# First feed-forward block: pairs 0 to 8 for each group alone, 9 to 21 for both groups by seven block products; three more convolution tiles on TensorE; the sums of one layer norm on VectorE

## The chip, the cores and the metric

One of the cores of a Trainium2 chip runs one inference step of a speech-encoder trunk. The metric is device time in microseconds (us) of one execution. The median of three runs before the change is 1541.64 us (1540.84 to 1542.74). One more execution was recorded by the profiler.

Engines: PE is TensorE (matrix products; its weight loads are shown as PEld), DVE is VectorE, ACT is ScalarE, POOL is GpSimd, SP is SyncE, which here only issues DMAs.

## The reference

640 columns (frames) of 1024 features: 128 of eight running streams ("sample") and 512 of one new stream ("prompt"). Layer 0 is a convolution module and a SwiGLU feed-forward block (FFN); layer 1 is attention on a shared key and value and a second FFN. What the change touches is layer 0:

```python
def swiglu_ffn(h, g, w_in, w_out):
    a, b = jnp.split(rms_norm(h, g) @ w_in, 2, axis=-1)
    return h + (jax.nn.silu(a) * b) @ w_out

def conv_module(h, hist, g, w_pw1, b_pw1, w_dw, b_dw, ln_g, ln_b, w_pw2, b_pw2):
    a, gate = jnp.split(rms_norm(h, g) @ w_pw1 + b_pw1, 2, axis=-1)
    glu = a * jax.nn.sigmoid(gate)
    full = jnp.concatenate([hist.astype(glu.dtype), glu], axis=1)
    y = lax.conv_general_dilated(
        full, w_dw[:, None, :].astype(full.dtype), window_strides=(1,), padding="VALID",
        dimension_numbers=("NWC", "WIO", "NWC"), feature_group_count=D_MODEL) + b_dw
    y = jax.nn.silu(layer_norm(y, ln_g, ln_b))
    return h + y @ w_pw2 + b_pw2, full[:, -CONV_HIST:]
```

The depthwise convolution has 31 taps. The hidden width is 2816 = 22 x 128, so an FFN has 22 "pairs": a pair is one 128-wide tile of `a` and the tile of `b` beside it, and needs 1 MB of `w_in`.

## The kernel before, in words

Features lie on the 128 partitions (8 tiles of 128), frames in the free dimension. The 640 columns are two groups: g0, the first 256 (the sample and 128 of the prompt), and g1, the other 384. Each group goes through the convolution module and the first FFN by itself, so that g0's FFN can run on PE while g1 is still in its convolution.

**Products.** All matrices are fp32, split in a high part `whi`/`xh` and a low part `wlo`/`xl`. `mm3` (L173) makes three matmuls for every 128x128 block: whi with xh, wlo with xh, whi with xl (L176 to L178). `wsplit` (L132) loads one weight tile of up to 1 MB through SP's queue, ACT copies it to `whi` (L156), and `wlo` = raw - `whi` is made at L160, by DVE, or by DVE and POOL: with pool=n, n quarters on POOL. `whi` and `wlo` have two buffers each. The raw tile has two buffers ("raw"), and every third load goes to a buffer of its own ("rx", tile pool `rxs`).

**FFN.** `ffn` (L327) runs chunks of pairs. `ffn_in` (L277) makes the two products of a pair and the gate, which leaves `hid` in both parts; after a chunk, `ffn_out` (L311) multiplies `hid` by the matching rows of `w_out`, and `out_tile` adds the result to the residual `h`. `FS` holds the chunks that g0 does alone: pairs 0 to 5, 6 to 11, 12 to 17. `FC` is the chunk for both groups with one weight tile (18 to 21). `FD` holds g1's chunks alone (0 to 17 once more, with the weights loaded a second time).

**Order of the convolution module.** The string `PLAN` (L72) is read token by token. Each token emits a step, the digit behind its letter is the group, the next ones are feature tiles: a and b make pw1 with GLU; l loads a convolution tile and p computes it on PE (`conv_pe_load` L448, `conv_pe` L465: 32 matmuls with 32 columns of weights; the input goes to DRAM as `sc` and comes back as `x4` through SP's queue; `w4` and `x4` have one buffer); d computes convolution tiles on DVE (`conv` L426, a scalar_tensor_tensor for each tap at L443, its accumulator in PSUM); q computes one by ACT's multiplies and POOL's adds (`conv_pool` L404, L422/L423); n is the layer norm over features (`conv_ln` L480); w is pw2; r is the RMS norm ahead of the FFN (`rms_late` L254); s writes convolution state out; f is one of `FS`'s chunks for g0. A step that stands later in the program is later on every engine's queue, unless `high_priority` lets it go ahead.

**The layer norm.** `colmean` (L192) adds the eight tiles up elementwise (L201 on POOL), then PE sums over partitions (L210) and `spread` (L216, L222) brings the mean to all partitions in PSUM. `conv_ln` subtracts the mean, squares, and does the same again for the variance; then it multiplies (L495), applies SiLU and splits into the parts that pw2 (w) multiplies.

**The second FFN** already works otherwise from its fourth pair on. With the 1024 features in two halves and the 640 columns in two halves of 320, a pair is a product of 2x2 blocks (of the weights: a's and b's halves; of the input: B11 to B22). The class `Unit` makes it by seven block products m1 to m7 instead of eight, with sums of weight blocks made on DVE and POOL (`prep`) and sums of input blocks (T1 to T4) made once. Each block product is 12 matmuls of 320 columns, so a pair takes 84; results are collected in PSUM banks pa, pb, pc, two of each.

## Time and profile before

| | us |
|---|---|
| median of three runs | 1541.64 (1540.84 to 1542.74) |
| the profiled execution's own time | 1541.31 |
| span of the profiled execution, first to last instruction | 1539.5 |
| PE busy | 1467.9 (95% of the span) |
| DVE busy | 1049.0 (68%) |
| ACT busy | 667.1 (43%) |
| POOL busy | 447.3 (29%) |
| granted TensorE clock, mean | 0.988 |

The profile is one execution on the chip. A row of the timeline or of the chain of waits has start and length in us, engine, the destination tile and line, operation, operand tiles and shapes, and in brackets how long the engine had been idle and what released it. Matmuls are pipelined: their listed lengths overlap, so the cost of one in a stream is the distance of two starts divided by the steps between them. "busy" of PE is therefore not work done at full speed.

### The profile page before, as it was taken

Reading aid. Unit: us, or ns where it says so; the run is one execution under the profiler, and the core shown is the slowest. Engines: PE = TensorE matmul, PEld = TensorE weight load, DVE = VectorE, ACT = ScalarE, POOL = GpSimd, SP = SyncE. Lnnn points to the kernel's source line nnn. Section 1 sums busy time; section 2 is a strip of 40 time slices with the busy share of each in tenths; the row PEclk is TensorE's granted clock in tenths of the full one; section 3 lists DMA queues with packets and bytes.
Section 4 is the critical chain, followed back from the end, with each engine's and each line's share of the span. In section 5 each row is a group of like instructions: output and inputs, shape, how many; then the busy total and the mean of one; then the engine's idle time right before and its main releaser. Section 6 shows DMA issues by size and latency. Waiting matters only on the chain.

```text
span 1539.5 us, 27212 instructions
## 1 busy us (share of the span) xinstructions
PE 1467.9 (95%) x11054; PEld 1397.9 (91%) x11054; DVE 1049.0 (68%) x1890; ACT 667.1 (43%) x1196; POOL 447.3 (29%) x406
## 2 busy tenths in 40 slices
PE   5988898989999999999999999999999999999998
PEld 5878878988999999999988798896989999999998
DVE  6994999989555444556577767666796467467456
ACT  4544455545423323235455445343564144244144
POOL 6965458987401000001322111110421011011010
PEclk9989899999999999999999999999999999999999
DMA  7884334454421333432555545444103222222222
GB/s 261 249 219 143 123 103 162 146 183 151 151 83 56 123 123 123 126 120 96 196 184 195 170 151 199 150 158 151 32 25 117 76 83 89 76 83 90 76 83 83
DMA packets 57022, 200.54 MB, mean 130 GB/s; under 512 B 10176, under 2 KB 20672, under 8 KB 44096
## 3 DMA queue, kind: packets, MB, share of 16 engines
q1 hardware_dynamic: 56608, 198.48, 39.1%
q8 instruction: 87, 1.43, 0.4%
q10 hardware_dynamic: 288, 0.31, 0.1%
q14 instruction: 39, 0.32, 0.1%
HBM read 187.55 MB, written 11.22 MB: 129 GB/s over the span
## 4 chain that ended last, share of the span: by engine, by line
PE 73%; DVE 15%; issue 3%; ACT 3%; POOL 3%; DMA 3%; SPq 0%; POOLq 0%; ACTq 0%; DVEq 0%
PE mm L176 13%; PE mm L177 13%; PE mm L178 13%; PE pb L977 6%; DVE w L443 4%; PE pc L977 4%; DVE wlo L160 4%; PE pa L977 3%; PE w L803 1%; PE pb L176 1%; PE pb L178 1%; PE pb L177 1%; PE pa L178 1%; PE pa L176 1%; PE pa L177 1%
## 5 line engine op out<-in xcount | busy, mean ns | idle before, releaser
L177 PE MATMUL mm<-x,wlo 128*128 128x256 f32 (+1 forms) x1344 | 417.8, 313 | 15.8 <-DVE wlo L160 15.4
L176 PE MATMUL mm<-x,whi 128*128 128x256 f32 (+1 forms) x1344 | 414.4, 312 | 9.2 <-ACT x L165 6.9
L178 PE MATMUL mm<-x,whi 128*128 128x256 f32 (+1 forms) x1344 | 413.0, 311 | 2.5 <-DVE x L166 2.5
L177 PEld LDWEIGHTS mm<-x,wlo 128*128 128x128 f32 x1344 | 257.1, 191 | 19.4 <-DVE wlo L160 18.3
L176 PEld LDWEIGHTS mm<-x,whi 128*128 128x128 f32 x1344 | 255.1, 191 | 14.1 <-ACT x L165 7.7
L178 PEld LDWEIGHTS mm<-x,whi 128*128 128x128 f32 x1344 | 255.3, 191 | 5.2 <-DVE x L166 4.1
L156 ACT ACTIVATE whi<-raw 128x2048 fp32r<-128x2048 f32 (+2 forms) x87 | 143.9, 1658 | 171.9 <-PE mm L178 105.1
L160 DVE TENSOR_TENSOR wlo<-raw,whi 128x2048 fp32r<-128x2048 f32 (+5 forms) x87 | 156.4, 1801 | 44.7 <-ACT whi L156 44.0
L922 POOL TENSOR_TENSOR raw<-raw 128x512 f32<-128x512 f32 x38 | 56.4, 1485 | 326.4 <-DVE raw L922 255.2
L177 PE MATMUL mm<-hid,wlo 128*128 128x256 f32 (+1 forms) x352 | 107.6, 308 | 6.1 <-DVE wlo L160 6.1
L160 POOL TENSOR_TENSOR wlo<-raw,whi 128x1536 fp32r<-128x1536 f32 (+3 forms) x33 | 93.0, 2822 | 55.1 <-ACT whi L156 55.1
L178 PE MATMUL mm<-hid,whi 128*128 128x256 f32 (+1 forms) x352 | 105.8, 307 | 0.8 <-DVE hid L166 0.7
L443 DVE SCALAR_TENSOR_TENSOR w<-gp,dwv,w 128x384 f32<-128x384 f32 x180 | 104.4, 613 | 0.9
L176 PE MATMUL mm<-hid,whi 128*128 128x256 f32 (+1 forms) x352 | 104.4, 307 | 0.0
L201 POOL TENSOR_TENSOR acc<-sq,sq 128x384 f32<-128x384 f32 (+1 forms) x8 | 8.1, 1006 | 255.8 <-ACT sq L185 255.8
L156 ACT ACTIVATE whi<-rx 128x2048 fp32r<-128x2048 f32 (+1 forms) x30 | 54.0, 1800 | 54.0 <-PE mm L178 42.0
L177 PEld LDWEIGHTS mm<-hid,wlo 128*128 128x128 f32 x352 | 66.0, 188 | 7.1 <-DVE wlo L160 7.1
L160 DVE TENSOR_TENSOR wlo<-rx,whi 128x2048 fp32r<-128x2048 f32 (+4 forms) x30 | 62.9, 2098 | 13.3 <-ACT whi L156 12.4
L423 POOL TENSOR_TENSOR y<-y,cvt 128x256 f32<-128x256 f32 (+1 forms) x60 | 67.9, 1132 | 4.3 <-ACT cvt L422 2.2
L178 PEld LDWEIGHTS mm<-hid,whi 128*128 128x128 f32 x352 | 65.7, 188 | 1.2 <-DVE hid L166 1.2
L176 PEld LDWEIGHTS mm<-hid,whi 128*128 128x128 f32 x352 | 65.1, 188 | 0.3 <-ACT hid L165 0.3
L165 ACT ACTIVATE whi<-raw 128x1024 fp32r<-128x1024 f32 x38 | 39.4, 1054 | 54.2 <-DVE raw L922 19.1
(329 smaller groups left out, 3648.2 us busy)
## 6 DMA issues: line engine op xcount, KB each, us to landing
raw<-in_w_in SPq DMA_DIRECT2D x49, 1024.0 KB
raw<-in_w_out SPq DMA_DIRECT2D x28, 768.0 KB
cache<-in_ck SPq DMA_DIRECT2D x32, 512.0 KB
cache<-in_cv SPq DMA_DIRECT2D x32, 512.0 KB
raw<-in_w_pw SPq DMA_DIRECT2D x14, 1024.0 KB
rx<-in_w_in SPq DMA_DIRECT2D x13, 1024.0 KB
rx<-in_w_pw SPq DMA_DIRECT2D x8, 1024.0 KB
raw<-in_w_kq SPq DMA_DIRECT2D x8, 1024.0 KB
```

Source lines behind the costliest of these rows:

```text
L156: nc.scalar.activation(out=hi[:, a:b], in_=raw[:, a:b], func=AF.Copy)
L160: eng.tensor_tensor(out=lo[:, a:b], in0=raw[:, a:b], in1=hi[:, a:b].bitcast(F32), op=ALU.subtract)
L165: nc.scalar.activation(out=hi, in_=src, func=AF.Copy)
L176: nc.tensor.matmul(ps, wh, xh, start=(i == 0), stop=False)
L177: nc.tensor.matmul(ps, wl, xh, start=False, stop=False)
L178: nc.tensor.matmul(ps, wh, xl, start=False, stop=(i == last))
L201: last["acc"] = eng.tensor_tensor(out=acc[:, :n], in0=prev, in1=s(), op=ALU.add)
L423: nc.gpsimd.tensor_tensor(out=y[g][:, c, :], in0=y[g][:, c, :], in1=pr[:, :n], op=ALU.add)
L443: nc.vector.scalar_tensor_tensor(out=dst, in0=src, scalar=wj, in1=dst, op0=ALU.mult, op1=ALU.add)
L803: nc.tensor.matmul(st[32 * b:32 * b + 32, 0:512], qv[b], KC[b // 2][:, b % 2, :], start=True, stop=True)
L922: ENG[e].tensor_tensor(out=out, in0=a, in1=b, op=op)
L977: nc.tensor.matmul(ps, a[:, c], b[:, k, :], start=(first and k == 0 and i == 0), stop=(k == 3 and i == 2), skip_group_check=not first)
```

## The change

- `FS` is (0,4), (4,4), (8,1): g0 alone does pairs 0 to 8. `FD` is (0,5), (5,4): g1 alone does the same pairs. `FC` is (9,5), (14,4), (18,4): 13 pairs for both groups, now by `Unit`, which moves up in the program and takes the weight tensor as an argument. The host swaps the halves of the b rows for pairs 9 and up.
- In `PLAN` g1's tile 6 leaves ACT and POOL (q16) and its tiles 2 and 7 leave DVE (d127); all three go to PE: l12 ahead of b6, p12 and l17 behind it, p17 and l16 behind the second pair of g0's first chunk and p16 behind its fourth. Two of g0's three lone chunks now stand ahead of g1's pw2 where three stood.
- `conv_ln` takes its sums' engine from `LE`: POOL for g0 as before, DVE for g1.
- g1's RMS norm keeps the products of gain and `h` in a tile `xg` (`keep=xg`). While g1's lone chunks run, they are multiplied there by the norm's factor, g0's normed columns are put beside them (the sum of the two parts of its input), and the blocks B11, B21, T1 to T3 are made from `xg`; B22 and T4 are made behind those chunks. Their tiles, `xe0`, `a22`, `xg0`, `tq0`, are allocated when the convolution's pools are closed, and the third raw buffer (`rxs`) is given up there, not at the end of the FFN.
- `bank()` in the first FFN takes the tag "mm", which has four PSUM banks; the second FFN has six.
- g1's lone chunks split 3/4 of `wlo` on POOL (`PFB`, where pool was 0); g0's do as before.

```diff
-FS = ((0, 6), (6, 6), (12, 6))
-FC = ((18, 4),)
-FD = ((0, 6), (6, 6), (12, 6))
+FS = ((0, 4), (4, 4), (8, 1))
+FC = ((9, 5), (14, 4), (18, 4))
+FD = ((0, 5), (5, 4))
...
+CHC = 5
...
-PLAN = ("a0 y a1 a2 a4 x a3 a5 a6 l04 p04 l05 d0213 a7 b0 p05 b1 l07 p07 l06 b2 q00 s0 p06 n0 b3 b4 b5 d145 l13 w0 b7 r0 p13 b6 f q16 s1 d101 d127 n1 f f w1 r1")
+PLAN = ("a0 y a1 a2 a4 x a3 a5 a6 l04 p04 l05 d0213 a7 b0 p05 b1 l07 p07 l06 b2 q00 s0 p06 n0 b3 b4 b5 d145 l13 w0 b7 r0 p13 l12 b6 p12 l17 s1 d101 f1p17.1l16.3p16 n1 f w1")
...
-    def rms_late(g, gain, engs=SQ, cut=CUT):
+    def rms_late(g, gain, engs=SQ, cut=CUT, keep=None):
...
-                t = tp.tile([P, 384], F32, tag="n1", name=nm("n1"), bufs=NB1)
+                t = (tp.tile([P, 384], F32, tag="n1", name=nm("n1"), bufs=NB1) if keep is None
+                     else keep[:, k, GR[g][0]:GR[g][0] + n])
...
+    def bank(tag=None):
+        if stage[0] == 0:
+            return mmt()
...
+    def units(src, js, where, chunks, u, hids, new_hid, outs):
+        for j in js:
+            c, jj = where[j]
+            w = None
+            if j + 1 < FT:
+                w = Unit(src, j + 1, hids[c], where[j + 1][1])
+                w.prep()
+                w.m1()
+            u.m7()
+            if w:
+                w.m5()
+            u.m3()
+            u.m4()
+            if w:
+                w.m6()
+                w.m2()
...
+    LE = (nc.gpsimd, nc.vector)
...
-        r, v = colmean(mu, [lambda c=c: y[g][:, c, :] for c in order], n, LCUT, "mst")
+        r, v = colmean(mu, [lambda c=c: y[g][:, c, :] for c in order], n, LCUT, "mst", LE[g])
...
-        bc, _ = rstd_bc([y[g][:, c, :] for c in order], n)
+        bc, _ = rstd_bc([y[g][:, c, :] for c in order], n, eng=LE[g])
...
     cv.close()
+    rxs.close()
+    third[1] = None
...
+    xs0, xs1 = late[0], rms_late(1, V_NFFN, keep=xg)
+    ffn({0: hp0}, w_in0, w_out0, {0: xs0}, (0,), chunks, PFB)
+    hid0.close()
     hid1 = ExitStack()
     hp1 = hid1.enter_context(tc.tile_pool(name="hp1", bufs=1))
-    ffn({0: hp0}, w_in0, w_out0, {0: xs0}, (0,), chunks, PFB)
-    if FC:
-        ffn({0: hp0, 1: hp1}, w_in0, w_out0, {0: xs0, 1: xs1}, (0, 1), FC)
-    ffn({1: hp1}, w_in0, w_out0, {1: xs1}, (1,), FD)
...
+    ffn({1: hp1}, w_in0, w_out0, {1: xs1}, (1,), FD[:1], PFB)
+    for k in range(KT):
+        add("v", xg[:, k, 0:256], xs0[0][:, k, :].bitcast(F32), xs0[1][:, k, :].bitcast(F32))
+        add("v", xg[:, k, 256:640], xg[:, k, 256:640], bca[:, 256:640], ALU.mult)
...
+    put4(B11, b11)
+    sub4(tq, b12, b11)
+    put4(T1, tq)
...
+    ffn({1: hp1}, w_in0, w_out0, {1: xs1}, (1,), FD[1:], PFB)
     hid1.close()
...
+    for f in (u.m1, u.m5, u.m6, u.m2):
+        f()
...
+    units(w_in0, range(FC[0][0], FT), pairs(FC), FC, u, hids, hid_c, outs0)
```

In the rows below, of each engine's queue in program order, a row has the line, the operation, destination and operand tiles, the operand's shape, and how often it stands there in a row. Lines of the changed kernel are one higher than before in this part of the program (L177 there is L176 before).

The first place is PE's queue between the second spread of g1's layer norm (`w2`, from `rst2`) and the first product of pw2 (operand `x`, 384 columns). Before, the spread stands among g0's output products (operand `hid`), and 84 rows lie between it and pw2:

```order
L176 MATMUL mm_507_4077<-hid_455_3624,whi_504_4051 128x256
L222 MATMUL w2_371_2981<-ident_78,rst2_382_3011 128x128 x3
L177 MATMUL mm_507_4077<-hid_455_3624,wlo_505_4052 128x256
L178 MATMUL mm_507_4077<-hid_455_3624,whi_504_4051 128x256
L176 MATMUL mm_507_4077<-hid_455_3624,whi_504_4051 128x256
```

Now pw2's first product stands straight behind it:

```order
L178 MATMUL mm_395_3207<-hid_353_2842,wlo_387_3104 128x256
L179 MATMUL mm_395_3207<-hid_353_2842,whi_386_3103 128x256
L223 MATMUL w2_332_2766<-ident_78,rst2_343_2796 128x128 x3
L177 MATMUL mm_399_3228<-x_344_2801,whi_397_3222 128x384
L178 MATMUL mm_399_3228<-x_344_2801,wlo_398_3223 128x384
L177 MATMUL mm_400_3254<-x_344_2801,whi_397_3222 128x384
```

The 84 products of g0 that stood behind the spread are ahead of it or after pw2, and pw2 starts with its high products.

The second place is where g1's squares (`sq`) are added up. Before, this is on POOL's queue, between its shares of `wlo`:

```order
L201 TENSOR_TENSOR acc_373_2984<-sq_372_2982,sq_374_2985 128x384
L160 TENSOR_TENSOR wlo_486_3879<-rx_484_3877,whi_485_3878 128x1536
L201 TENSOR_TENSOR acc_373_2984<-acc_373_2984,sq_375_2988 128x384
L201 TENSOR_TENSOR acc_373_2984<-acc_373_2984,sq_376_2991 128x384
L160 TENSOR_TENSOR wlo_493_3942<-raw_491_3940,whi_492_3941 128x1536
L201 TENSOR_TENSOR acc_373_2984<-acc_373_2984,sq_377_2994 128x384
```

Now it is on DVE's queue, between DVE's shares of `wlo` and g0's gates (`t2`, `hid`):

```order
L161 TENSOR_TENSOR wlo_384_3097<-raw_382_3095,whi_383_3096 128x512
L202 TENSOR_TENSOR acc_334_2769<-sq_333_2767,sq_335_2770 128x384
L167 TENSOR_TENSOR hid_353_2842<-t2_374_3027,hid_353_2842 128x256
L296 TENSOR_TENSOR t2_381_3090<-t1_380_3089,mm_379_3064 128x256
L202 TENSOR_TENSOR acc_334_2769<-acc_334_2769,sq_336_2773 128x384
L202 TENSOR_TENSOR acc_334_2769<-acc_334_2769,sq_337_2776 128x384
L161 TENSOR_TENSOR wlo_387_3104<-raw_385_3102,whi_386_3103 128x512
L167 TENSOR_TENSOR hid_353_2842<-t2_381_3090,hid_353_2842 128x256
```

The adds moved from POOL to DVE; POOL keeps its 1536 columns of each `wlo`.

The third place is PE's queue in the pairs for both groups. Before, pair 18 begins with three matmuls for each feature tile, `x_256` being g0's input:

```order
L176 MATMUL mm_575_4629<-x_256_2036,whi_573_4624 128x256
L177 MATMUL mm_575_4629<-x_256_2036,wlo_574_4625 128x256
L178 MATMUL mm_575_4629<-x_256_2036,whi_573_4624 128x256
L176 MATMUL mm_576_4654<-x_256_2036,whi_573_4624 128x256
L177 MATMUL mm_576_4654<-x_256_2036,wlo_574_4625 128x256
```

Now a piece of the block pairs reads as follows; `mm_581` is the bank pc of one pair and ends with its m3, `mm_585` is the same pair's pb in m4, and `mm_598` is the next pair's pb, which m6 begins:

```order
L373 MATMUL mm_594_4986<-xe0_3464,wlo_589_4943 128x320
L373 MATMUL mm_594_4986<-xe0_3464,whi_588_4942 128x320
L373 MATMUL mm_581_4863<-x1c_4609,bk_577_4821 128x320 x7
L373 MATMUL mm_598_5034<-xe0_3464,whi_588_4942 128x320
L373 MATMUL mm_585_4911<-x1c_4609,bk_577_4821 128x320 x12
L373 MATMUL mm_598_5034<-xe0_3464,wlo_589_4943 128x320
L373 MATMUL mm_598_5034<-xe0_3464,whi_588_4942 128x320 x2
```

The 256- and 384-column products of such a pair (96) became 84 of 320 columns. With four banks in rotation, `mm_598` takes the bank of `mm_581`, and its first product stands right behind the last one into that bank; this neighbourhood is in 4 of the 13 pairs.

More of the change, by code (lines that the diff above doesn't have):

```diff
@@ new lines, in tmp, with add, copy, prod @@
+    def tmp(t):
+        if stage[0] == 0 and t == "t3":
+            t = "n1"
+        return tp.tile([P, 384], F32, tag=t, name=nm(t))[:, 0:HT]
+    def add(e, out, a, b, op=ALU.add):
+        ENG[e].tensor_tensor(out=out, in0=a, in1=b, op=op)
+    def copy(out, src):
+        nc.scalar.activation(out=out, in_=src, func=AF.Copy)
+    def prod(ps, w, x, first):
+        wh, wl = w
+        xh, xl = x
+        for k in range(4):
+            c = slice(k * P, (k + 1) * P)
+            for i, (a, b) in enumerate(((wh, xh), (wl, xh), (wh, xl))):
+                nc.tensor.matmul(ps, a[:, c], b[:, k, :], start=(first and k == 0 and i == 0),
+                                 stop=(k == 3 and i == 2), skip_group_check=not first)
@@ L339, in tile_trunk, with pairs @@
+    def pairs(chunks):
+        return {j0 + jj: (c, jj) for c, (j0, ch) in enumerate(chunks) for jj in range(ch)}
     hid0 = ExitStack()
@@ L524, in step, with hook @@
     def step(op, arg):
+        if op == "f":
+            def hook(jj):
+                for t in arg.split("."):
+                    if t and int(t[0]) == jj:
+                        step(t[1], t[2:])
+            ffn({0: hp0}, w_in0, w_out0, {0: late[0]}, (0,), (chunks.pop(0),), PFA, hook=hook)
+            return
         g, cs = int(arg[:1] or 0), [int(c) for c in arg[1:]]
@@ new lines, in tile_trunk, with put4, sub4 @@
+    hb = half_blocks(xe, 7) + half_blocks(cst.tile([P, 2 * KT * 256], F32R, tag="x0", name="x0c"), 3)
+    xc = [None] * 7
+    for i, b in enumerate((B11, T1, T2, B21, T3)):
+        xc[b] = hb[2 * i], hb[2 * i + 1]
+    (b11, b12), (b21, b22) = [[xg[:, 4 * q:4 * q + 4, c] for c in TH] for q in range(2)]
+    def put4(i, src):
+        for k in range(4):
+            xsplit(src[:, k, :], xc[i][0][:, k, :], xc[i][1][:, k, :])
+    def sub4(out, a, b):
+        for k in range(4):
+            add("v", out[:, k, :], a[:, k, :], b[:, k, :], ALU.subtract)
@@ new lines, in tile_trunk, with outs0 @@
+    hb = half_blocks(cst.tile([P, 2 * KT * 384], F32R, tag="x1", name="x1c"), 4)
+    xc[B22], xc[T4] = (hb[0], hb[1]), (hb[2], hb[3])
+    u = Unit(w_in0, FC[0][0], hids[0], 0)
+    u.prep((a22[:, 0:512], a22[:, 512:1024]))
+    with tc.high_priority(offset=HP):
+        put(B22, b22)
+        put(T4, tq)
+    xgs.close()
+    wfs = ExitStack()
+    wf = wfs.enter_context(tc.tile_pool(name="wf0", bufs=2, side="right"))
+    u.prep_back()
+    for f in (u.m1, u.m5, u.m6, u.m2):
+        f()
+    def outs0(c):
+        j0, ch = FC[c]
+        ffn_out(w_out0, j0, ch, {g: (hids[c][:, 0, :, TG[g]], hids[c][:, 1, :, TG[g]])
+                                 for g in range(2)}, (0, 1), 0)
@@ L898, in tile_trunk @@
     xg = [xg[:, 0:4], xg[:, 4:8]]
-    ENG = {"v": nc.vector, "p": nc.gpsimd}
-    B11, B21, B22, T1, T2, T3, T4 = range(7)
-    banks = [0]
-    def bank(tag=None):
-        if tag is None:
-            tag = ("pa", "pb", "pc")[banks[0] % 3]
-            banks[0] += 1
-        return mm.tile([P, 512], F32, tag=tag, name=nm(tag))
+    stage[0] = 1
     proj_o(NP // 2 - 1)
@@ L969, in plain @@
             gate(ps[0], ps[1], hids[0], jj, c)
-    def prod(ps, w, x, first):
-        wh, wl = w
-        xh, xl = x
-        for k in range(4):
-            c = slice(k * P, (k + 1) * P)
-            for i, (a, b) in enumerate(((wh, xh), (wl, xh), (wh, xl))):
-                nc.tensor.matmul(ps, a[:, c], b[:, k, :], start=(first and k == 0 and i == 0),
-                                 stop=(k == 3 and i == 2), skip_group_check=not first)
-    def quarter(hi, lo, i):
-        return hi[:, 512 * i:512 * i + 512], lo[:, 512 * i:512 * i + 512]
@@ L1185, in tile_trunk @@
         put(T4, tq)
-    where = {}
-    for c, (j0, ch) in enumerate(F1):
-        for jj in range(ch):
-            where[j0 + jj] = c, jj
     xgs.close()
```

241 lines of the change are left out of this document (126 added, 115 removed).

## The prediction

> **What bounds the kernel now.** I read first the chain of waits by engine, then windows around the changed part, then PE's waits in it, then single rows.
>
> ```profile
> PE 73%; DVE 15%; issue 3%; ACT 3%; POOL 3%; DMA 3%; SPq 0%; POOLq 0%; ACTq 0%; DVEq 0%
> ```
>
> PE sets most of the end, DVE a seventh. The share says nothing about where, so I cut the first FFN by its stages. These three rows are the marks: the first product of g0's first pair, the product behind pw2 of g1 (w1 below), and the first product behind the whole first FFN.
>
> ```profile
> 207.06 0.28 PE L176 MATMUL mm<-x,whi 128*128 128x256 f32 x1
> ...
> 419.82 0.28 PE L176 MATMUL mm<-x,whi 128*128 128x256 f32 x1
> ...
> 731.02 0.36 PE L176 MATMUL mm<-x,whi 128*128 128x256 f32 x1 [1.30 <-DVE h L309]
> ```
>
> ```profile
> core 0: us, PE busy (x) PEld busy (x) DVE busy (x) ACT busy (x) POOL busy (x), PEclk, DMA share, GB/s
> 207.00:333.00 126.00, 110.62 (x901) 107.02 (x900) 125.75 (x206) 64.97 (x87) 106.59 (x55) 0.97 0.46 151
> 333.00:384.00 51.00, 47.62 (x411) 47.03 (x411) 42.37 (x49) 26.17 (x36) 39.83 (x20) 1.00 0.46 151
> ...
> 420.00:731.00 311.00, 309.72 (x1892) 309.41 (x1892) 164.19 (x219) 107.85 (x147) 16.06 (x16) 1.00 0.32 106
> ```
>
> ```profile
> engine line waited for: us in total, times, longest us
> PE mm L177 <- DVE wlo L160: 17.8, 16, 2.6
> ```
>
> The first window is DVE's: 125.75 of 126 us busy, and PE waits in 211 to 420 us for DVE's low parts 16 times, 17.8 us. Behind 420 us it is PE's: 309.72 of 311. So the change has two kinds of gain: load taken from DVE and POOL before 420 us, and PE work saved behind it. Here is what fills DVE, and what fills POOL between 207 and 385 us:
>
> ```profile
> L443 DVE SCALAR_TENSOR_TENSOR w<-gp,dwv,w 128x384 f32<-128x384 f32 x134 | 76.0, 611 | 0.2
> L160 DVE TENSOR_TENSOR wlo<-raw,whi 128x512 fp32r<-128x512 f32 x9 | 15.8, 1757 | 0.0
> ...
> L423 POOL TENSOR_TENSOR y<-y,cvt 128x384 f32<-128x384 f32 x30 | 36.7, 1223 | 0.9
> ```
>
> **PE's prices.** In a stream of matmuls the distance of starts counts, so here are the ends of a run of 384 columns (15 steps), of one of 256 (36 steps), a block product of the second FFN's pairs, and two pieces of one convolution tile of g1.
>
> ```profile
> 400.26 0.34 PE L178 MATMUL mm<-x,whi 128*128 128x384 f32 x1
> ...
> 402.88 0.34 PE L178 MATMUL mm<-x,whi 128*128 128x384 f32 x1
> ...
> 480.42 0.28 PE L178 MATMUL mm<-hid,whi 128*128 128x256 f32 x1
> ...
> 484.50 0.28 PE L178 MATMUL mm<-hid,whi 128*128 128x256 f32 x1
> ...
> 1252.31 3.52 PE pb L977 x24
> ...
> 192.41 3.43 PE L475 MATMUL mm<-x,w 128*32 128x384 f32 x40
> ...
> 196.41 2.14 PE L475 MATMUL mm<-x,w 128*32 128x384 f32 x24
> ```
>
> That is 0.1747 us for 384 columns, 0.1133 for 256, 0.1467 for 320. A plain pair for both groups is 48 x (0.1133 + 0.1747) = 13.82; a block pair is 84 x 0.1467 = 12.32. **13 block pairs save 13 x 1.50 = 19.5.** The output products keep their columns. A pair that the groups make apart costs PE what it costs when both make it together, so only the blocks save. A convolution tile of g1 on PE is 3.43 + 2.14 = 5.57; three **add 16.7**. PE's own work thus falls by 2.8 only, and nearly all of a gain must come from waits.
>
> The Trainium skill, page "TensorE: Matmul & The Clock Gate", section "Back-to-back issue gap", gives about 81 ns a matmul with its weight load for 128 columns and 131 for 512. Read in between, an estimate, that would be 98, 114 and 106 ns for 256, 384 and 320 columns, 1.27 us a pair and 16.5 in all, 3 less than above; the rows' 113, 175 and 147 disagree with it, and the rows decide.
>
> **Before, 207 to 420 us.** 212.8 us of wall. Of products there are 18 pairs x 48 x 0.1133 = 97.9, their output 18 x 24 x 0.1133 = 48.9, w1 8 x 24 x 0.1747 = 33.5, sums and spreads about 3: 183.4. So 29.4 are over pure work, 17.8 of them the waits above.
>
> **After, DVE's part.** The convolution of g1 on DVE loses tiles 2 and 7, 60 of the 134 rows at L443.
>
> ```profile
> 216.06 2.19 DVE L443 SCALAR_TENSOR_TENSOR w<-gp,dwv,w 128x384 f32<-128x384 f32 x4
> ...
> 274.46 3.24 DVE L443 SCALAR_TENSOR_TENSOR w<-gp,dwv,w 128x384 f32<-128x384 f32 x6
> ...
> 330.23 1.92 DVE L443 SCALAR_TENSOR_TENSOR w<-gp,dwv,w 128x384 f32<-128x384 f32 x3
> ```
>
> From 216.1 some 69 are left, each 3.24 / 6 = 0.54: 37.3. Between them stand seven low parts of 1.76 (12.3), and 18 gate and output operations and five adds of the norm of about 0.45 (10.4, by the rows of 0.41 and 0.51 below), 2 more for stretched ones: the convolution and the sum of its tiles end near **278**, instead of 332 us.
>
> **After, PE's part to the norm's sums.** Ahead of them stand three convolution tiles 16.7, six pairs 32.6, the first chunk's output 96 x 0.1133 = 10.9, and 21 products 2.4: 207.1 + 62.6 = 269.7. Now SP's queue. The changed order puts p12's `x4` behind a 1 MB weight, and `x4`'s single buffer makes l17's load wait until p12 is done, l16's until p17, with weights queued behind both. The nearest case in the trace, of p07:
>
> ```profile
> 108.90 1.73 SPq L461 DMA_DIRECT2D x<-sc  x4
> ...
> 117.95 3.66 PE L475 MATMUL mm<-x,w 128*32 128x256 f32 x64 [0.52 <-DMA x<-sc]
> ```
>
> Nine us pass from issue to use there. For p12 the bounds are 0 (landed in time) and 9 (nothing hides it); I take 4, since b6's product covers about half. Low parts late in the first chunk: bounds 0 and 17.8 by the old waits, I take 3, because DVE has less between them. PE comes to the sums at 277, DVE at 278: nearly balanced.
>
> **After, norm chain and w1.** The chain before, and its last links:
>
> ```profile
> 361.14 2.30 POOL L201 TENSOR_TENSOR acc<-acc,sq 128x384 f32<-128x384 f32 x2
> ...
> 369.81 0.72 PE L210 MATMUL w<-onec,acc 128*128 128x1 f32 x6
> 374.75 0.83 PE L222 MATMUL w<-ident,rst 128*128 128x128 f32 x6
> 375.61 3.81 DVE L495 TENSOR_TENSOR y<-y,w 128x384 f32<-128x384 f32 x8 [0.71 <-PE w L222]
> ...
> 380.00 2.05 DVE L160 TENSOR_TENSOR wlo<-raw,whi 128x384 fp32r<-128x384 f32 x1
> 381.97 1.02 DVE L166 TENSOR_TENSOR x<-n,x 128x384 fp32r<-128x384 f32 x2
> ```
>
> Squares are added on DVE now, 1.02 / 2 = 0.51 each where POOL takes 2.30 / 2 = 1.15. PE's queue has 167 products of g0 between the first sums and the second spread: 18.9, and 2.4 for sums and spreads. For waits there (output weights' split, adds, the power) I take 4, between 0 and the 21 more of the first rival below. The spread is done at 278 + 18.9 + 2.4 + 4 = 303. Then nothing of g0 covers: the order has w1 straight behind. Eight multiplies 3.81, a low part 2.05 and the first split about 0.45 are 6.3; w1's eight high products cover 8 x 0.1747 = 1.4, so 4.9 stay open. w1 starts at 308 and ends at 308.2 + 33.5 = **341.7, 78 earlier than the old 419.82**.
>
> **After, the rest.** From 419.82 to 731.02 the old kernel has 311.2. The new one has ten pairs of g0's side still to do: 10 x (48 + 24) x 0.1133 = 81.6 more, blocks 19.5 less. Preparing B11 to T4 adds DVE and ACT work, which the window behind 420 hides: DVE 164.19 and ACT 107.85 of 311. If it were not hidden it would cost at most DVE's some 50 operations x 0.5 = 25. Low parts move 3/4 to POOL there, busy 16.06. The third raw buffer goes; the same window shows DMA at a share of 0.32, so I put that at 0, at worst the old 17.8 of weight waits. Four banks for six: the price is ACT's SiLU, which must empty a bank.
>
> ```profile
> L1057 ACT ACTIVATE t<-pc x19: 437/438/441, 1160.5 to 1508.2; 128x320 f32<-128x320 f32 x19
> ```
>
> Where m6's first product stands straight behind m3 in its bank, PE waits 0.44 and some latency, about 0.7: four pairs, 2.8. Changes of chunk and the start of the blocks about 2. Together 5; bounds 0 and 13 x 1.5 = 19.5, which would eat the blocks. Sum: 341.7 + 311.2 + 81.6 - 19.5 + 5 = **720**, 11 before 731.02. Behind that both kernels run the same instructions in the same order on PE. The profiled execution took 1541.31 (median of the runs 1541.64, so either serves): 1541.3 - 11.2 = **1530**. A measurement can tell about 0.2%, 3 us, from no change.
>
> **The rivals.** *The chain stays long (slower).* Before, from the convolution's end at 332.1 to w1's start (419.8 - 33.5 = 386) it took 54 us, of which g0's products covered nearly all. Now cover is about 23 (18.9 + 2.4 + 1.4). Why it could stay long is seen here: a POOL low part, and DVE operations beside it and without it.
>
> ```profile
> 336.99 3.98 POOL L160 TENSOR_TENSOR wlo<-raw,whi 128x1536 fp32r<-128x1536 f32 x1 [0.70 <-ACT whi L156]
> ...
> 337.55 3.70 DVE L166 TENSOR_TENSOR hid<-t,hid 128x256 fp32r<-128x256 f32 x1
> ...
> 247.82 0.41 DVE L166 TENSOR_TENSOR hid<-t,hid 128x256 fp32r<-128x256 f32 x1
> ```
>
> DVE's operation with both inputs in SBUF waits for POOL's whole one: 3.70 for 0.41. The adds moved to DVE are of just that kind. With a chain of about 51 from 278, w1 starts at 329, 21 later: 1530 + 21 = **1551**. It becomes slower than before from a chain of about 41 (w1 at 319). For it: the lock, with low parts of three pairs and an output in the chain. Against it: POOL has lost 36.7 us of q16 and all of the chain's adds, and DVE its 60 taps. 18%.
>
> [...]
>
> *Four banks, or the blocks' extra transformations, eat the saving (about same).* Each block pair takes 13.8 or so: 14.5 more, **1545**. For: DVE and ACT must empty every bank at once. Against: the second FFN's rows show no wait of PE with six banks, and the order has tight reuse in 4 of 13. 14%.
>
> *PE-bound throughout (faster).* The window to w1 costs only some 6 over pure work: 16.7 + 8 x 48 x 0.1133 + 192 x 0.1133 + 33.5 + 3 = 118.5, so w1 ends at 331, and with 2 lost behind it instead of 5 the end comes 13 earlier: **1517**. For: DVE and POOL both lose load. Against: the chain must fit under 23. 18%.
>
> **How the numbers follow.** The forecast, 1530, has 50%. Faster: forecast and the last rival, 68%. The bank rival lies on the bound between no change and slower, split 11 and 3; with the first rival slower is 21%. The range runs from 1517 to 1549: below it and above it half of the outer rivals.
>
> **What would show it.** Right: w1's last product near 342, 720 for the product now at 731.02, DVE's convolution ended at 275 to 278, block pairs every 12.3 to 12.9 us, p12 waiting some 4 us for `x4`. Wrong: DVE's adds of the norm at 2 to 4 us instead of 0.5, over 20 us of PE waits between the convolution and w1, waits of m6 for ACT in most pairs, or weight loads late for want of the third buffer.

## The result, and the profile after

The changed kernel takes 1555.01 us (median of 5 runs, 1553.20 to 1560.82), the kernel before 1542.74 beside it. The ratio is 1.0085, 95% interval 1.0056 to 1.0113: **slower by about 13 us**, where 11 us faster was forecast. The profiled execution took 1553.47 us with a span of 1551.7. All five runs lie above the upper end of the range, 1549.

First the chain of waits by engine of the changed kernel. As before, it says little about the place:

```profile
PE 71%; DVE 16%; ACT 4%; issue 3%; DMA 3%; POOL 2%; SPq 0%; POOLq 0%; DVEq 0%; ACTq 0%
```

Then the marks, from the timelines of the changed kernel: the sum of the last convolution tile, the second spread of g1's norm, the first product of pw2 (w1), the product behind w1, the first block product, and the first product behind the first FFN (kq).

```profile
274.02 0.56 DVE L202 TENSOR_TENSOR acc<-acc,y 128x384 f32<-128x384 f32 x1 [0.94 <-ACT y L600]
...
305.47 0.83 PE L223 MATMUL w<-ident,rst 128*128 128x128 f32 x6
...
309.29 0.44 PE L177 MATMUL mm<-x,whi 128*128 128x384 f32 x1 [2.99 <-ACT x L166]
...
345.39 0.28 PE L177 MATMUL mm<-x,whi 128*128 128x256 f32 x1
...
480.72 0.31 PE L373 MATMUL mm<-xe,whi 128*128 128x320 f32 x1
...
740.91 0.36 PE L177 MATMUL mm<-x,whi 128*128 128x256 f32 x1 [2.84 <-DVE rst L233]
```

Up to w1's end the forecast holds: convolution 274.5 (278 forecast), spread 305 (303), w1 from 309.3 to 345.4 (308.2 to 341.7). Then 395.5 us pass to kq's first product where 378.3 were forecast, and kq starts at 740.9 instead of 720. Most of the miss lies behind w1. Windows of the changed kernel by stage (front, lone pairs, blocks with their outputs; columns as in the prediction's windows):

```profile
207.00:345.40 138.40, 125.59 (x991) 113.92 (x984) 119.00 (x191) 55.58 (x73) 68.01 (x25) 0.98 0.39 117
...
345.40:480.70 135.30, 125.81 (x733) 123.65 (x733) 101.54 (x140) 55.28 (x74) 61.82 (x22) 1.00 0.37 122
480.70:737.50 256.80, 253.47 (x1718) 251.13 (x1717) 164.81 (x248) 103.93 (x178) 46.42 (x36) 1.00 0.24 81
```

And of the kernel before, behind w1:

```profile
420.00:480.00 60.00, 60.00 (x428) 60.00 (x428) 29.82 (x45) 21.48 (x33) 2.83 (x2) 1.00 0.21 72
480.00:731.00 251.00, 249.72 (x1467) 249.41 (x1466) 134.37 (x175) 86.37 (x114) 13.23 (x14) 1.00 0.34 114
```

Before, PE was never idle in the 60 us behind w1. Now the stage with the lone pairs has 9.5 us without PE (135.30 - 125.81), with DVE busy 101.5 of 135 and POOL 61.8 where it was almost free. By the prediction's prices this stage is one pair of g0 (72 x 0.1133 = 8.2) and nine of g1 (9 x 72 x 0.1747 = 113.2): 121.4. It takes 135.3, so 13.9 over. PE's waits in it, in the changed kernel (total, times, longest), and below the dots those of the block stage and of kq's start:

```profile
PE mm L178 <- DVE wlo L161: 3.9, 2, 3.4
PE mm L177 <- DVE t L300: 2.6, 1, 2.6
PE mm L179 <- DVE hid L167: 1.6, 1, 1.6
PE w L211 <- POOL acc L202: 1.3, 1, 1.3
...
PE mm L177 <- DVE rst L233: 2.8, 1, 2.8
PE mm L373 <- ACT acc L365: 1.6, 1, 1.6
PE mm L373 <- ACT whi L166: 1.4, 3, 0.6
```

The largest two of the lone pairs, each with DVE's and POOL's row at that time:

```profile
356.93 3.44 POOL L161 TENSOR_TENSOR wlo<-raw,whi 128x1536 fp32r<-128x1536 f32 x1 [2.48 <-ACT whi L157]
356.96 3.95 DVE L161 TENSOR_TENSOR wlo<-raw,whi 128x512 fp32r<-128x512 f32 x1
360.97 0.44 PE L178 MATMUL mm<-x,wlo 128*128 128x384 f32 x1 [3.45 <-DVE wlo L161]
...
372.57 3.79 POOL L161 TENSOR_TENSOR wlo<-raw,whi 128x1536 fp32r<-128x1536 f32 x1 [8.30 <-ACT whi L157]
373.37 3.33 DVE L167 TENSOR_TENSOR x0c<-xg,xe 128x320 fp32r<-128x320 f32 x1
380.44 0.44 PE L177 MATMUL mm<-x,whi 128*128 128x384 f32 x1 [2.62 <-DVE t L300]
```

A quarter of a low part takes DVE 3.95 us while POOL's three quarters run (it takes 0.69 elsewhere), and a split of a block input takes 3.33 for 0.48; g1's gate stands behind it and 3.1 us more of block inputs in DVE's queue, and PE waits for that gate's bank. The Trainium skill, page "SBUF — State Buffer", section "Who interferes with whom", states that a VectorE instruction with two SBUF inputs contends with a GpSimd instruction that reads SBUF, by a lock for the whole instruction; these pairs of rows agree.

The end of the stage has a wait that the kernel before did not have in this size. DVE's queue and PE's next products there, in the changed kernel:

```profile
737.61 2.69 DVE L167 TENSOR_TENSOR x<-h,x 128x384 fp32r<-128x384 f32 x3
740.22 0.54 DVE L311 TENSOR_TENSOR h<-mm,h 128x384 f32<-128x384 f32 x1
740.69 0.14 DVE L233 TENSOR_SCALAR rst<-w 128x2 f32<-128x2 f32 x1
...
742.09 0.41 PE L178 MATMUL mm<-x,wlo 128*128 128x256 f32 x1
742.30 0.41 PE L179 MATMUL mm<-x,whi 128*128 128x256 f32 x1
```

g0's and g1's last outputs now come together at the end, so both norms ahead of kq lie open: three splits of 0.9 us stand before DVE's last add, and PE waits 2.84 us. Shortly behind it, from 741.45 to 744.86, the products come every 0.21 us instead of 0.1133.

### The profile page after: what moved, and what is told of

It reads as the page before. It is cut to its first block, busy times and chain, and to the rows that moved or that the text cites. A ratio compares the mean times of both kernels' runs of the same rounds, so it can differ in the third digit from the quotient of the medians.

```text
span 1551.7 us, 27359 instructions
## 1 busy us (share of the span) xinstructions
PE 1471.1 (95%) x11090; PEld 1387.4 (89%) x11090; DVE 1087.3 (70%) x1982; ACT 669.5 (43%) x1238; POOL 445.7 (29%) x392
## 4 chain that ended last, share of the span: by engine, by line
PE 71%; DVE 16%; ACT 4%; issue 3%; DMA 3%; POOL 2%; SPq 0%; POOLq 0%; DVEq 0%; ACTq 0%
PE mm L177 10%; PE mm L178 10%; PE mm L179 10%; PE mm L373 9%; PE pb L373 6%; PE pc L373 4%; PE pa L373 4%; DVE w L597 3%; DVE wlo L161 3%; PE w L1032 1%; PE pb L177 1%; PE pb L178 1%; PE pb L179 1%; ACT whi L157 1%; PE pa L179 1%
## 5 line engine op out<-in xcount | busy, mean ns | idle before, releaser
L177 PE MATMUL mm<-x,whi 128*128 128x256 f32 (+1 forms) x928 | 290.2, 316 | 16.3 <-ACT x L166 9.9
L178 PE MATMUL mm<-x,wlo 128*128 128x256 f32 (+1 forms) x928 | 291.0, 315 | 9.7 <-DVE wlo L161 9.3
L179 PE MATMUL mm<-x,whi 128*128 128x256 f32 (+1 forms) x928 | 286.2, 313 | 2.1 <-DVE x L167 2.1
L177 PEld LDWEIGHTS mm<-x,whi 128*128 128x128 f32 x928 | 177.8, 193 | 22.9 <-ACT x L166 10.8
L178 PEld LDWEIGHTS mm<-x,wlo 128*128 128x128 f32 x928 | 178.6, 193 | 12.7 <-DVE wlo L161 11.5
L179 PEld LDWEIGHTS mm<-x,whi 128*128 128x128 f32 x928 | 176.8, 192 | 4.8 <-DVE x L167 3.6
L157 ACT ACTIVATE whi<-raw 128x2048 fp32r<-128x2048 f32 (+3 forms) x77 | 123.8, 1612 | 124.2 <-PE mm L179 62.8
L161 DVE TENSOR_TENSOR wlo<-raw,whi 128x512 fp32r<-128x512 f32 (+7 forms) x77 | 129.8, 1689 | 35.0 <-ACT whi L157 34.5
L161 POOL TENSOR_TENSOR wlo<-raw,whi 128x1536 fp32r<-128x1536 f32 (+4 forms) x39 | 113.8, 2921 | 133.2 <-ACT whi L157 126.3
L167 DVE TENSOR_TENSOR wlo<-raw,whi 128x1024 fp32r<-128x1024 f32 x64 | 85.1, 1341 | 11.2 <-ACT whi L166 10.4
L373 PE MATMUL mm<-xe,whi 128*128 128x320 f32 x364 | 88.8, 310 | 2.9 <-ACT acc L365 1.6
L177 PE MATMUL mm<-hcc,whi 128*128 128x256 f32 (+1 forms) x208 | 63.7, 308 | 0.2 <-DVE h L311 0.2
L179 PE MATMUL mm<-hcc,whi 128*128 128x256 f32 (+1 forms) x208 | 63.1, 308 | 0.0
```

The costliest lines, as they stand in the source:

```text
L157: nc.scalar.activation(out=hi[:, a:b], in_=raw[:, a:b], func=AF.Copy)
L161: eng.tensor_tensor(out=lo[:, a:b], in0=raw[:, a:b], in1=hi[:, a:b].bitcast(F32), op=ALU.subtract)
L167: nc.vector.tensor_tensor(out=lo, in0=src, in1=hi.bitcast(F32), op=ALU.subtract)
L177: nc.tensor.matmul(ps, wh, xh, start=(i == 0), stop=False)
L178: nc.tensor.matmul(ps, wl, xh, start=False, stop=False)
L179: nc.tensor.matmul(ps, wh, xl, start=False, stop=(i == last))
```

## The experiments

Each ratio is to the kernel before, run beside it. Lines named below are those of the changed kernel; in experiments 9 and 13, which alter the kernel before, they are those of that kernel.

| kernel | ratio | 95% interval |
|---|---|---|
| the change | 1.0085 | 1.0056 to 1.0113 |
| 1: g1's lone low parts on DVE | 1.0041 | 1.0022 to 1.0061 |
| 2: plain pairs for both groups | 1.0164 | 1.0143 to 1.0185 |
| 3: norm's sums on POOL | 1.0145 | 1.0124 to 1.0166 |
| 4: tile 6 on ACT and POOL | 1.0189 | 1.0168 to 1.0209 |
| 5: experiment 1, three more lone pairs | 1.0212 | 1.0189 to 1.0235 |
| 6: experiment 1, second chunk on DVE | 1.0090 | 1.0062 to 1.0119 |
| 7: experiment 1, second output on DVE | 1.0060 | 1.0040 to 1.0080 |
| 8: experiment 1, no cover behind w1 | 1.0109 | 1.0081 to 1.0137 |
| 9: before, with the front alone | 1.0066 | 1.0046 to 1.0086 |
| 10: experiment 7, later norms' sums on DVE | 1.0038 | 1.0020 to 1.0057 |
| 11: old front, four blocks | 1.0102 | 1.0080 to 1.0124 |
| 12: old front, five blocks | 1.0173 | 1.0145 to 1.0200 |
| 13: before, with the order alone | 1.0067 | 1.0039 to 1.0094 |

From this profile the theory was that PE waits in g1's lone pairs for DVE operations that POOL's low parts hold up. The rivals were that the tiles on PE, the blocks, or the norm's sums on DVE are the loss.

### 1. Low parts of g1's lone pairs on DVE

```diff
-    ffn({1: hp1}, w_in0, w_out0, {1: xs1}, (1,), FD[:1], PFB)
+    ffn({1: hp1}, w_in0, w_out0, {1: xs1}, (1,), FD[:1], 0)
...
-    ffn({1: hp1}, w_in0, w_out0, {1: xs1}, (1,), FD[1:], PFB)
+    ffn({1: hp1}, w_in0, w_out0, {1: xs1}, (1,), FD[1:], 0)
```

> The changed kernel, but g1's lone pairs and their output weights make their low parts on VectorE alone, as before the change. Theory (waits in g1's lone pairs, made by GpSimd's low parts that VectorE's two-SBUF operations wait for): the five PE waits of 1.2 to 3.5 us between w1's end and the first block product, 9.5 us together in the changed kernel, fall to under 4, that stage (345.4 to 480.7, 135.3 us) gets 5 to 9 us shorter, the whole about 1548. Rival (VectorE is simply too full there, with the blocks' inputs made beside the gates): a whole low part of about 2.2 us in place of 0.7 makes the stage as long or longer, the whole 1553 to 1560.

1549.16 us. The window of the same stage:

```profile
348.70:478.90 130.20, 125.48 (x734) 124.01 (x733) 91.42 (x140) 55.85 (x74) 8.21 (x7) 0.99 0.38 126
```

PE's waits in it:

```profile
PE mm L178 <- DVE wlo L161: 2.6, 2, 2.0
PE w L211 <- POOL acc L202: 1.4, 1, 1.4
PE mm L179 <- DVE hid L167: 0.6, 1, 0.6
```

DVE makes four times the columns and is busy 10 us less: what fell is the time that it was held up. A whole low part of 2048 columns takes it 2.28 us without POOL, the quarter beside POOL took 3.95:

```profile
361.74 2.28 DVE L161 TENSOR_TENSOR wlo<-raw,whi 128x2048 fp32r<-128x2048 f32 x1
```

The stage is 5.1 us shorter, the whole about 6 (1.0085 to 1.0041; the intervals overlap by a little). The theory holds for about half of the loss. 4.6 us of waits stay, more than the "under 4" expected.

### 2. No blocks

The 13 pairs as plain pairs for both groups behind g1's lone ones, without block inputs.

```diff
...
+    ffn({1: hp1}, w_in0, w_out0, {1: xs1}, (1,), FD, PFB)
+    ffn({0: hp0, 1: hp1}, w_in0, w_out0, {0: xs0, 1: xs1}, (0, 1), FC)
```

> The changed kernel with the 13 pairs for both groups as plain pairs: no block products, no sums of input blocks. Convolution, norm and the lone pairs stay as changed. Theory (blocks save about what PE's prices say, 19.5, and give some 10 back by their inputs' preparation and waits): 10 us slower than the changed kernel, about 1565. Rival (the blocks' preparation and their four PSUM banks eat the whole saving): as long as the changed kernel, 1552 to 1557, and the loss against before comes from the front alone. Rival 2 (blocks cost nothing beside): 1573 or more.

1568.31 us, so the blocks are worth 12 us (1.0164 to 1.0085). The windows of its lone pairs and of its pairs for both groups:

```profile
348.30:481.90 133.60, 126.94 (x734) 125.96 (x733) 81.61 (x95) 43.14 (x48) 58.06 (x20) 0.97 0.39 128
481.90:755.80 273.90, 271.01 (x1877) 270.92 (x1876) 118.96 (x180) 77.56 (x124) 11.56 (x13) 1.00 0.23 76
```

From the first of these pairs to kq's first product are 273.9 us here and 260.2 (740.91 - 480.72) with blocks: 13.7 of the forecast 19.5. The rival that the blocks eat their own saving falls. The lone stage is nearly as long as in the changed kernel (133.6 to 135.3), though no block input is made in it, so the making of the inputs isn't the main cause. It isn't shown to be free: PE is idle for 6.7 us in this window instead of 9.5, and the granted clock is 0.97 instead of 1.00, which alone can be up to 4 us.

### 3. The norm's sums on POOL

```diff
-    LE = (nc.gpsimd, nc.vector)
+    LE = (nc.gpsimd, nc.gpsimd)
```

> The changed kernel with the sums of g1's layer norm on GpSimd as before. Theory (the moved adds were a help: six or seven at 0.55 us instead of 1.1 to 2.3 on GpSimd, beside its low parts): the second spread comes 5 to 12 us after the changed kernel's 305.5, the whole is 3 to 10 us slower, 1558 to 1565. Rival (the two-SBUF adds on VectorE were held up by GpSimd and cost as much): no difference, 1553 to 1557, or faster.

1564.29 us. The second spread comes at 310.3, w1 ends at 356.5, 11 later. PE's longest wait in the front:

```profile
PE w L211 <- POOL acc L202: 7.2, 1, 7.2
```

This part of the change is worth 9 us in this kernel.

### 4. Tile 6 on ACT and POOL

```diff
-... s1 d101 f1p17.1l16.3p16 n1 f w1
+... s1 d101 f1p17 q16 n1 f w1
```

> The changed kernel with g1's convolution tile 6 back on ScalarE and GpSimd (q16); tiles 2 and 7 stay on PE. PE has 5.6 us less to do before the norm, GpSimd some 37 more between its low parts. Theory (the front is balanced between PE and VectorE, and GpSimd has room there, busy 26 to 37 of 73 us): the first sums come at the same time, since VectorE's convolution ends at 274 either way, and the rest of PE's products move ahead of them: 0 to 5 us faster than the changed kernel, 1550 to 1555. Rival (GpSimd's adds hold up its low parts and VectorE's gates, as before the change): w1 ends 5 to 20 us later, the whole 1560 or more.

1571.74 us: the rival. w1 ends at 363.2, 18 later. PE stands waiting for the norm's sums:

```profile
PE w L211 <- DVE acc L202: 13.8, 2, 8.8
PE mm L178 <- DVE wlo L161: 8.0, 6, 3.7
```

So with nine lone pairs tile 6 is better on PE. Whether the tiles pay beside 18 is the ninth experiment.

### 5 to 8. Cover and locks around w1

All four on top of experiment 1.

```diff
5:
-FS = ((0, 4), (4, 4), (8, 1))
-FC = ((9, 5), (14, 4), (18, 4))
-FD = ((0, 5), (5, 4))
+FS = ((0, 4), (4, 4), (8, 4))
+FC = ((12, 5), (17, 5))
+FD = ((0, 6), (6, 6))
...
6, in step f:
-(chunks.pop(0),), PFA, hook=hook)
+(chunks.pop(0),), PFA if arg else 0, hook=hook)
...
7, in ffn:
-ffn_out(w_out, j0, ch, hid, og or groups, pl)
+ffn_out(w_out, j0, ch, hid, og or groups, 0 if j0 == 4 and 0 in groups else pl)
...
8, in PLAN:
-n1 f w1
+n1 f f w1
```

> The first experiment's kernel (g1's lone low parts on VectorE) with three pairs less in blocks: FS (0,4), (4,4), (8,4), FC (12,5), (17,5), FD (0,6), (6,6). g0 thus has four lone pairs behind pw2 instead of one, 33 us of cover instead of 8. Blocks save 10 x 1.5 instead of 13 x 1.5: 4.5 us lost. Theory (after w1 the changed kernel stalls because too little of g0 covers g1's RMS norm, the first low parts of g1 and the blocks' inputs): the PE waits between w1's end and the first block product, 5.2 us in the first experiment with the slower clock behind them, fall under 1.5, and the sum is 0 to 3 us better than the first experiment, ratio to before 1.002 to 1.004. Rival (these waits have other causes, the VectorE queue in g1's own pairs): they stay, and the ratio goes up by the 4.5 us, to about 1.007.

1572.68 us, ratio 1.0212: worse than either side expected. From w1's end to the first block, PE waits for g0's own added pairs:

```profile
PE mm L179 <- DVE hid L167: 4.9, 2, 3.7
PE mm L178 <- DVE wlo L161: 3.0, 2, 2.4
PE mm L177 <- DVE t L296: 2.1, 1, 2.1
```

They kept 3/4 of their low parts on POOL, and a pair of g0 is only 48 x 0.1133 = 5.4 us of PE work for 1 MB of weights. As cover they need low parts and gates from DVE, the operations that are held up. The theory that more of g0's pairs behind w1 would repair the loss falls as far as these are split in this way; with their low parts on DVE it wasn't tried.

> The first experiment's kernel, and g0's second lone chunk (pairs 4 to 7 and their output, beside the norm of g1) makes its low parts on VectorE alone. Theory (the norm's chain is stretched by GpSimd's low parts: two hid operations of 3.6 us instead of 0.4 and 9 us of PE waits from 276 to 312): the chain from VectorE's last convolution to w1's first product, 35 us in the changed kernel, gets 3 to 6 us shorter; the whole 2 to 6 us faster than the first experiment, ratio about 1.001. Rival (VectorE is the bound until its convolution ends, and each low part costs it 1.5 us more): the convolution ends 3 to 5 us later and eats that, ratio 1.004 to 1.007.

1552.84 us: the rival, and by more than it said. The convolution's last add comes at 283.3 instead of 275.7 in experiment 1, w1 starts at 313.6 instead of 310.9. The theory's part came too: from that add to w1 it takes 30.3 us instead of 35.2. The 7.6 us by which the convolution ends later outweigh the 4.9.

> The first experiment's kernel, and only the output weights of g0's second lone chunk, which fall in the norm's chain, make their low parts on VectorE alone; its pairs keep 3/4 on GpSimd. Theory (locks in the chain): the hid operation of 3.67 us and the waits of 2.6 and 1.4 us near 295 go, w1 starts 2 to 4 us earlier, ratio about 1.002. Rival (two low parts of 2.2 us on VectorE stand in the chain themselves): no change, ratio 1.004.

1549.23 us. The waits for hid are gone and w1 starts at 305.6, 5.3 earlier than in experiment 1 (2 to 4 expected), but the ratio (1.0040 to 1.0080) can't be told from experiment 1's. What was gained in the place isn't shown in the whole.

> The first experiment's kernel with g0's third lone chunk (pair 8 and its output, 8.2 us) ahead of pw2 of g1 instead of behind it. Theory (both places need cover): the gap of 3.8 us between the second spread and w1's first product goes, and behind w1 nothing of g0 covers g1's RMS norm and first low part, whose waits grow from 4 to 6 to 12 us: 2 to 8 us slower than the first experiment, ratio 1.006 to 1.009. Rival (only the gap ahead of w1 matters, g1's pairs don't wait for the norm since it is applied behind the products): 3 to 5 us faster, ratio about 1.001.

1556.50 us, ratio 1.0109: slower, as the theory said, but not in the place that it named. Behind w1 the stage to the first block takes 123.2 us (361.87 to 485.03); in experiment 1 it took 130.2 with the 8.2 us of g0 in it, so 122.0 without. PE's waits there are 4.8 us, of them 2.4 for the split of g1's input, where 12 were expected. Ahead of w1's end 13.2 us were added (361.87 to 348.66) for 8.2 us of work: PE waits 2.8 us for pair 8's hid, 2.5 for a low part inside w1, and the granted clock from 318 to 333 us is 0.66. So g0's products stood better behind w1; that they cover the norm there isn't shown.

### 9. The front alone

The kernel before with the changed convolution plan and norm sums; FS, FC, FD and the plain pairs as before.

```diff
-... b7 r0 p13 b6 f q16 s1 d101 d127 n1 f f w1 r1
+... b7 r0 p13 l12 b6 p12 l17 s1 d101 f1p17.1l16.3p16 n1 f f w1 r1
```

> The kernel before, with only the changed convolution and norm: g1's tiles 2, 7 and 6 on PE, the norm's sums on VectorE. All 18 lone pairs of g0 stay ahead of pw2, no blocks. PE has 16.7 us more work than before. Theory (moving the tiles buys away VectorE's waits, but those were 17.8 us, so it can only about pay for itself; what makes the changed kernel slow is the thin cover behind it): the stretch from g0's first pair to w1's end stays within 5 us of before's 212.8, the whole 1537 to 1547. Rival (the tiles on PE are the loss): the stretch gets 10 to 17 us longer, the whole 1552 to 1559.

1554.04 us, ratio 1.0066. In the profiled execution, the longest of the seven (1558.92), w1 ends at 433.9 instead of 419.8, 14 later, for 16.7 us more of PE work. PE's waits there:

```profile
PE mm L177 <- DVE wlo L160: 5.7, 3, 3.2
PE w L210 <- DVE acc L201: 3.8, 1, 3.8
PE mm L178 <- DVE hid L166: 1.6, 2, 1.5
```

The 17.8 us of waits for low parts became 5.7, and others came in: with those below the three rows, PE waits 15.4 in all. The rival holds: with 18 pairs of cover the tiles on PE are work added, and PE's idle time falls by little, from 18.8 us (207 to 420 before) to 15.5.

### 10. Later norms' sums on DVE

On top of experiment 7; `rms_late` gets an engine for its sums, and g0's third chunk makes its low parts on DVE.

```diff
-    xs0, xs1 = late[0], rms_late(1, V_NFFN, keep=xg)
+    xs0, xs1 = late[0], rms_late(1, V_NFFN, keep=xg, eng=nc.vector)
...
-    xs = [rms_late(0, None), rms_late(1, None)]
+    xs = [rms_late(0, None, eng=nc.vector), rms_late(1, None, eng=nc.vector)]
```

> The kernel of the seventh experiment, and GpSimd leaves three more places: the low parts of g0's third lone chunk, and the sums of squares of g1's RMS norm ahead of the FFN and of both norms behind it, are made on VectorE. Theory (GpSimd's two-SBUF operations hold up VectorE's queue: after w1, and at the end of the first FFN, where three splits of 0.9 us stand ahead of the add for which PE waits 2.9): PE's wait ahead of kq falls under 1.5 us, those after w1 under 3, the whole 3 to 6 us faster than the seventh, ratio about 1.002 to 1.004. Rival (VectorE's queue is long there anyway, its own 21 adds of 0.5 us make it longer): waits stay or grow, ratio 1.006 or more.

1549.21 us, ratio 1.0038. The wait ahead of kq is nearly gone:

```profile
737.40 0.35 PE L177 MATMUL mm<-x,whi 128*128 128x256 f32 x1 [0.49 <-DVE h L311]
```

DVE's splits there take 0.51 to 0.55 us where the three in the changed kernel took 0.90 each, so POOL's adds were what held them up. Behind w1 a wait of 3.3 us, now for ACT's whi, took the place of those removed, against the expected "under 3". The median is that of the seventh experiment (1549.23); the ratios' intervals overlap, so a gain over it isn't shown. Among all versions tried this one and experiment 1 are the fastest with blocks, and both are slower than before.

### 11 and 12. Old front with a few blocks

PLAN as before the change up to w1; FS, FC and FD cut at pair 18 (11, sums on POOL) and at pair 17 (12, sums on DVE), blocks only behind it. g1's lone low parts are on DVE.

```diff
-FS = ((0, 4), (4, 4), (8, 1))
-FC = ((9, 5), (14, 4), (18, 4))
-FD = ((0, 5), (5, 4))
+FS = ((0, 6), (6, 6), (12, 6))
+FC = ((18, 4),)
+FD = ((0, 6), (6, 6), (12, 6))
```

> The front of the kernel before (tiles 2 and 7 on VectorE, 6 on GpSimd, sums on GpSimd, 18 lone pairs of g0 ahead of pw2), and only its four pairs for both groups as block products; g1's lone low parts on VectorE as before. Blocks save 4 x 1.5 = 6.0 on PE. Theory (the loss of the changed kernel comes from the tiles on PE and the thin cover, not from the blocks): w1 ends within 3 us of before's 419.8, g1's lone pairs, now straight behind it, cost 5 to 7 us of waits as in the eighth experiment, the end of the first FFN's norm 3: ratio 0.999 to 1.003. Rival (the block stage itself costs, by its inputs and its start): ratio 1.005 or more.

1557.71 us, ratio 1.0102. w1 starts at 385.0, as before the change (386.1). From there to kq's first product it takes 358.8 us instead of 344.9, 13.8 more, although four blocks save 6. Neither the tiles on PE nor a thin cover ahead of w1 are in this kernel: what is left is the blocks' making, the third raw buffer given up early, or the order that blocks need, g1's lone pairs first.

> The eleventh experiment's kernel with one lone pair less (17; five blocks) and the norm's sums on VectorE. Theory (before, 11 us of g0's products stood between the norm's second spread and w1, and the sums on VectorE shorten the chain by 5 or more, so one pair of 8.2 us can leave the cover): w1 ends 5 to 8 us earlier than in the eleventh, and one more block saves 1.5; since that pair's g0 side comes later, the whole is 0 to 2 us faster than the eleventh. Rival (the chain binds already): w1 ends where it did, and the whole is 5 to 8 us slower than the eleventh.

1568.75 us, 11 slower than the eleventh and worse than the rival said. w1 starts at 390.8, 5.8 later than in the eleventh, although one pair less stands ahead of it.

### 13. The order alone

```diff
-    if FC:
-        ffn({0: hp0, 1: hp1}, w_in0, w_out0, {0: xs0, 1: xs1}, (0, 1), FC)
     ffn({1: hp1}, w_in0, w_out0, {1: xs1}, (1,), FD)
+    ffn({0: hp0, 1: hp1}, w_in0, w_out0, {0: xs0, 1: xs1}, (0, 1), FC)
```

> The kernel before, with one thing changed: g1's 18 lone pairs run ahead of the four pairs for both groups (plain) instead of behind them, which is the order that block products need, since their inputs take g1's input's place. Theory (this order is the loss of the eleventh experiment: g1's lone pairs stand straight behind pw2 and wait for the split of their input and for low parts, and g0's norm ahead of kq, covered by g1's last pairs before, is laid open): waits of 6 us or more between w1 and the first pair for both groups, 3 or more ahead of kq, the whole 8 to 16 us slower than before, ratio 1.005 to 1.010. Rival (the order costs nothing; the blocks' inputs and start are the loss of the eleventh): ratio 0.998 to 1.002.

1552.36 us, ratio 1.0067. PE's waits from w1's end to kq's first product; the kernel before has only 1.3 us there:

```profile
PE mm L176 <- DVE rst L232: 2.9, 1, 2.9
PE mm L176 <- ACT x L165: 2.4, 1, 2.4
PE w L210 <- POOL acc L201: 0.8, 1, 0.8
```

Moving one line costs about 10 us (6 to 14.5 by the interval). kq starts 10.7 us later (741.73 to 731.02). Of these, 3.0 stood already at w1's start (389.1 to 386.1), up to which the two programs are the same, so they aren't put down to the order. From w1's start to kq it takes 352.6 us instead of 344.9, 7.7 more. The waits there are 6.1 against 1.3: between w1 and the pairs for both groups 3.2 with the sums, and at kq 2.9. Behind the first of them the products slow down: from 425 to 437 us the granted clock is 0.72, an estimate of 3.4 us lost (12 x 0.28). Wait and slow products together make the 6 that was expected behind w1.

So the order stands for 7.7 of the eleventh's 13.8 us; the other 6, and the 6 that its blocks should have saved, it doesn't explain. The eleventh's trace has two things that this one lacks: w1 takes 40.0 us instead of 33.7, with a wait of 3.3 for a low part and a granted clock of 0.57 from 404 to 412 us; and most products of g1's 18 lone pairs come 0.1767 us apart instead of 0.1733, which over 18 x 72 of them is up to 4.4 us. No run takes these apart.

## Why the prediction was wrong

**The front (w1's end at 341.7).** The walk was right to 3.7 us (345.4), in part by luck. The wait of p12 for `x4` was 0.59 and p16's 1.40, 2.0 together where 4 stood. The convolution ended 3.5 earlier and the chain behind it took 34.8 (274.5 to 309.3) where 30.2 stood; the two nearly cancel. w1 itself took 36.1 instead of 33.5, with the granted clock at 0.57 from 311 to 315. The first rival, a chain of about 51, didn't come: the adds on DVE took 0.55 to 0.56 each, and experiment 3 shows that they help by 9 us. But in the forecast's own sum the front was no gain either: 78.1 earlier, 81.6 still to do. The ninth experiment, with 18 lone pairs, shows it as a cost of 10 us.

**The step that failed is "The rest".** It took the old kernel's 311.2 us behind w1 with its almost unbroken PE, added pairs and subtracted the blocks' saving. That window was unbroken because of an order that the change reverses: both groups' pairs straight behind w1, g1's last. Allowed for this was "changes of chunk and the start of the blocks about 2". Measured over pure work: lone pairs 13.9, blocks and outputs 6.7 (256.8 to 13 x 12.32 + 89.9 for outputs), kq's start 3.4, 24.0 in all; 6.8 were in the sum (5, and 1.9 that the old window held over its own products). The difference, 17.2, is nearly the whole miss; the front's 3.7 is the rest of the 21 by which kq's start was missed.

**"The window behind 420 hides" the blocks' inputs.** DVE's 164 of 311 is a mean. In 345 to 481 it is 101.5 of 135.3, in a queue that runs in order, and "low parts move 3/4 to POOL there" was entered at nothing although the prediction's own rows (3.70 for 0.41) priced it: it costs about 6 us (experiment 1). DVE held up by POOL was looked for in the norm and not behind it.

**The blocks (19.5).** The mechanism was right, the size too large: 13.7 in the traces of the change and experiment 2, 12 in the medians. PE's waits in the block stage are 3.3 us of the shortfall; with them the blocks come to 17.0, and the rest isn't taken apart. No row shows the SiLU as releaser, so the 2.8 set aside for it, and the second rival's cause, fall. The longest of the waits, 1.55 at 614.90, is for a copy by ACT that stands behind a high part (613.47), which itself had waited 1.40 for its weight to land. So the third raw buffer, or something else that makes a weight late, was not quite the 0 of the sum; no run tests it alone.

By the Trainium skill's page "TensorE: Matmul & The Clock Gate", section "Back-to-back issue gap", read in between, the estimate had been 16.5, from 98, 114 and 106 ns a product; the trace's 113 to 118, 173 to 177 and 147 don't agree with these.

**Nothing stood in the sum for g0's norm ahead of kq.** Before, g1's 18 lone pairs ran over it; now it lies open, 3.4 us with the sums. The slow products behind it don't count against the change: the kernel before has such a stretch there too, with a granted clock of 0.89 from 731 to 746 as the changed one from 740.9 to 756. Of the 12.2 us by which the span is longer, 9.9 stand at kq's first product; the 2.3 behind it aren't taken apart.

The loss, put together from kernels that were run: the front alone 10 us, the order alone 10, both with the lone pairs cut to nine 25 (experiment 2), the blocks 12 back, 13 in all. The two parts that cost were meant to make room for the part that pays. The 5 us between 20 and 25 are not taken apart, and the intervals (4 us or so on each 10) leave room for them. One candidate is known: experiment 2 keeps 3/4 of g1's lone low parts on POOL, experiments 9 and 13 don't, and experiment 1 puts that at about 6.

## What to carry to other kernels

A stage that runs without waits owes it to what stands beside it. When its neighbours change, price the stage anew from queue orders, not by adding to and subtracting from its old length. Ask of a faster product what order it demands, and run that order alone first: here one moved line alone costs about 10 us. A mean occupancy of an in-order engine doesn't hide a burst, least of all beside an engine that holds it up.
